# Placing the split activations of a down projection by a stepped offset, and reading part of its weights in interleaved chunks

## The chip, the cores and the metric

The kernel runs on one core of one Trainium2 chip. The metric is the device time of one execution in microseconds (us). Three executions of the kernel before took 2352.05, 2350.78 and 2352.41 us; their median is 2352.05 us.

## The reference

One layer of a diffusion backbone runs over 384 tokens (128 of a prompt and 256 latent ones) of 2048 channels: a mixer with three branches, then a gated feed-forward block whose hidden width is 5632. The change is in the last product of that block, the down projection, and in where the tiles behind it lie:

```python
h2 = rmsnorm(x, norm_ffn_pre) * (1 + sc2) + sh2
u, g = jnp.split(h2 @ w_ffn_up, 2, axis=-1)
g = along_cols(lambda t: dwconv(t, ffn_conv_w, ffn_conv_b), g, rows)
f = (jax.nn.gelu(g) * u) @ w_ffn_down
x = x + g2 * rmsnorm(f, norm_ffn_post)
```

All values are 32-bit floats. The kernel reaches the accuracy of a float32 product with three passes: an operand x is split into a rounded part hi and a rest lo, and a product is taken as hi·hi + lo·hi + hi·lo, each pass in the type fp32r.

## The kernel before

A long list of weight pieces is worked through in order (`run_stream`). Each piece of the down projection is one DMA of 128 rows by 1024 columns into a buffer `raw`. ScalarE (ACT) writes its rounded part `whi` and VectorE (DVE) its rest `wlo` (L164 and L165, in the helper `split`); three buffers of each take turns. Splits run two pieces ahead of the matmuls.

The down projection is the last stage. It has two halves of 1024 output columns (h = 0, 1), and in each half 44 steps (k = 0 to 43), one for each block of 128 hidden channels: 88 steps, numbered s = 44h + k. In a step the block `fx[k]` (128 channels by 384 tokens) is split into hi and lo as well (`down_split`, L1502 before), two steps ahead; here these are called the split activations. Then there are 18 matmuls: three groups of 128 tokens (t), two blocks of 512 columns (b), and three passes (L1512, L1513, L1514 before). In each the stationary operand, which a weight load (LDWEIGHTS, engine name PEld) brings into the array, is a 128x128 piece of the split activations, and the moving operand is 512 columns of `whi` or `wlo`. The sum stays in six PSUM banks over the 44 steps of a half. The last three steps of the second half (s = 85, 86, 87) are held back and run group by group in `down_last`, so that the work on a finished group (`down_out`, `down_finish`) runs beside the matmuls of the next one.

Where operands lie: the pool `hp` has 16 slots `hx0` to `hx15`, each a tile of 772 elements (3088 bytes) in every partition. In the built programs, before and after alike, neighbouring slots lie 3104 bytes apart, which is 32 bytes more than a multiple of 512. The buffers `whi` and `wlo` lie at multiples of 512 bytes from each other and from slot `hx0`. Before the change the split activations of step s are one tile in slot `hx{s % 3}`, with hi at its start and lo 1536 bytes (three times 512) behind it. So hi and lo of a step have the same place within 512 bytes, and against the weights that place is 0, 32 or 64 bytes on, by s % 3. "Offset" below means this: the address of the stationary operand less that of the moving one, within 512 bytes. It never changes within a step.

The stages before it run the other way round: in the input and up projections the stationary operand is a piece of `whi` or `wlo`, and the moving one is hi or lo of a normalised activation tile in slot `hx{k}`, k = 0 to 15 (L173, L174, L175). There the offset goes through 16 values that are 32 bytes apart, with the lo part 8 bytes further on. In the branch product that reads the tile `hc` all offsets are 0.

At the end of a half `down_out` squares each of the six PSUM banks into a scratch tile and multiplies it by a gain into a tile `fo` (128x512). Before, the twelve `fo` tiles of the two halves take slots `hx3` to `hx14`.

Of the kernel before, what the change touches and what calls it, by code (L numbers as in the profile page):

```python
# [12 lines left out]
F32 = mybir.dt.float32  # L13
F32R = mybir.dt.float32r
# [5 lines left out]
P = 128  # L20
# [4 lines left out]
NT = SEQ + LAT  # L25
HW = NT + 2
# [9 lines left out]
NF = DFF // P  # L36
# [10 lines left out]
NB = 512  # L47
# [45 lines left out]
def body(ctx: ExitStack, tc: tile.TileContext, i, o):  # L93
    nc = tc.nc
    ctx.enter_context(tc.manual_schedule())
    act, dve, pe, sync, gp = nc.scalar, nc.vector, nc.tensor, nc.sync, nc.gpsimd
# [10 lines left out]
    hp = ctx.enter_context(tc.tile_pool(name="hp", bufs=1, side="left"))  # L107
# [5 lines left out]
    def name(base):  # L113
        uid[0] += 1
        return f"{base}{uid[0]}"

    def bank(b, shape=(P, 512)):
        return psp.tile(list(shape), F32, name=name("ps"), tag=f"bank{b}")
# [44 lines left out]
    def split(hi, lo, src):  # L163
        act.activation(hi, src, AF.Copy)  # L164
        dve.tensor_sub(lo, src, hi.bitcast(F32))  # L165
# [126 lines left out]
    def sqrt_table():  # L292

        act.activation(tmp("dm", 1, bufs=1), eps, AF.Sqrt)
# [58 lines left out]
    hx = [None] * KD  # L353
# [4 lines left out]
    def h_pair(tag, n):  # L358

        t = hp.tile([P, 2, n], F32R, name=name("hx"), tag=tag)  # L360
        pr = Two()
        pr.hi, pr.lo = t[:, 0], t[:, 1]
        return pr
# [929 lines left out]
    F = {}  # L1293
# [167 lines left out]
    fo = {}  # L1461
# [30 lines left out]
    def g2_load(h):  # L1492
        t = F["p"].tile([P, 2, HALF_D], F32, name=name("gb"), tag="gb")
        for c in range(2):
            gp.dma_start(t[:, c], G2D[c : c + 1, HALF_D * h : HALF_D * (h + 1)].broadcast_to([P, HALF_D]))
        DN["g", h] = t

    def down_start():
        down_split(0)
        down_split(1)  # L1500

    def down_split(s):  # L1502
        if s >= 2 * NF:
            return
        pr = h_pair(f"hx{s % 3}", NT)
        split(pr.hi, pr.lo, fx[s % NF])
        DN["f", s] = pr

    def down_mm(ps, x, hi, lo, t, b, first, last):
        xh, xl = x.hi[:, t * P : (t + 1) * P], x.lo[:, t * P : (t + 1) * P]  # L1510
        w = slice(b * NB, (b + 1) * NB)
        pe.matmul(ps, xh, hi[:, w], start=first, stop=False, skip_group_check=True)  # L1512
        pe.matmul(ps, xl, hi[:, w], start=False, stop=False, skip_group_check=True)  # L1513
        pe.matmul(ps, xh, lo[:, w], start=False, stop=last, skip_group_check=True)  # L1514

    def down_use(h, k):
        def f(hi, lo):
            if k == 0:
                acc4 = [(rot["acc"] + c) % 4 for c in range(1, 5)]
                free = [4, 5, 6, 7] + acc4[:2] if h == 0 else acc4[2:] + [4, 5, 6, 7]  # L1520
                DN["ps", h] = [bank(b) for b in free]
            ps = DN["ps", h]
            x = DN.pop(("f", h * NF + k))
            down_split(h * NF + k + 2)
            if h == 1 and k >= NF - 3:
                DN["last"] = DN.get("last", []) + [(k, hi, lo, x)]
                if k == NF - 1:
                    down_last(ps)
                return
            for t in range(3):  # L1530
                for b in range(2):
                    down_mm(ps[2 * t + b], x, hi, lo, t, b, k == 0, k == NF - 1)
                if k == NF - 1:
                    for b in range(2):
                        down_out(h, t, b, ps[2 * t + b])
            if k == NF - 1:
                g2_load(1)
                sqrt_table()

        return f  # L1540

    def down_out(h, t, b, ps):

        n = 2 * h + b
        junk = hp.tile([P, NB], F32, name=name("junk"), tag="hx15")
        act.activation(junk, ps, AF.Square, accum_out=ss4[:, t, n : n + 1])
        g = hp.tile([P, NB], F32, name=name("fo"), tag=f"hx{3 + 4 * t + n}")
        dve.tensor_mul(g, ps, DN["g", h][:, min(t, 1), b * NB : (b + 1) * NB])
        fo[t, n] = g

    def down_last(ps):

        for t in range(3):
            for b in range(2):
                for k, hi, lo, x in DN["last"]:
                    down_mm(ps[2 * t + b], x, hi, lo, t, b, False, k == NF - 1)
                down_out(1, t, b, ps[2 * t + b])
                if b == 0:

                    sp = sp4[:, t : t + 1]  # L1560
                    dve.tensor_add(sp, ss4[:, t, 0:1], ss4[:, t, 1:2])
                    dve.tensor_add(sp, sp, ss4[:, t, 2:3])
                    dve.tensor_scalar(sp, sp, 1.0 / D, EPS, ALU.mult, ALU.add)
            if t:
                down_finish(t - 1)
        down_finish(2)
# [139 lines left out]
```

## Time and profile before

| | |
|---|---|
| median of three runs | 2352.05 us |
| the profiled execution's own time | 2352.14 us |
| its span, first to last instruction | 2350.4 us |
| mean granted TensorE clock | 0.995 |
| PE busy | 2312.1 us, 12597 matmuls |
| DVE busy, ACT busy | 1490.0 us, 933.8 us |
| down projection, matmuls L1512 to L1514 | 3 x 528, from 1970.4 to 2338.3 us |
| behind its last matmul | 12 us |

A timeline row has the start in us, the duration in us, the engine, the line, the operation and its tiles. Matmuls overlap in the records: one of 512 columns is recorded with 0.39 to 0.40 us, but the next begins about 0.23 us after it. So the time that a matmul costs is the distance between starts, called its **pitch** below, and not its recorded duration. Of a group, "x528 | 208.0, 394" means 528 instructions, 208.0 us in which at least one was busy, and 394 ns as the mean duration.

### The profile page before, as it was taken

How to read it: one execution, taken by the hardware profiler on the slowest of the kernel's cores; microseconds unless marked ns; L12 is line 12 of the kernel's file. 1: busy time of each engine (PE TensorE's matmuls, PEld its weight loads, DVE VectorE, ACT ScalarE, POOL GpSimd, SP SyncE). 2: the span in 40 equal slices, each digit the busy share in tenths (PEclk: the TensorE clock that was granted, in tenths of full speed). 3: DMA queues.
4: the chain of work that ended last, by engine and by line, in shares of the span. 5: the costliest groups of instructions: out<-in, count | busy, mean ns of one | idle time of the engine just before them, and what ended most of it. 6: DMA issues, size and time to landing. Idle time of an engine off the chain costs nothing.

```text
span 2350.4 us, 32026 instructions
## 1 busy us (share of the span) xinstructions
PE 2312.1 (98%) x12597; PEld 2189.8 (93%) x12597; DVE 1490.0 (63%) x2286; ACT 933.8 (40%) x1417; POOL 33.0 (1%) x72
## 2 busy tenths in 40 slices
PE   7999999999999999999999999999999999999997
PEld 3899999999999999999999999999999999888886
DVE  6876777646788777868556577776444445444444
ACT  6853333434322232324356533333333334334333
POOL 0000000000000000000000000000000000000000
PEclk9999999999999999999999999999999999999999
DMA  9954334234566666667533355554343333334332
GB/s 342 326 159 143 100 119 128 95 112 156 193 219 222 223 219 231 229 201 276 190 90 126 122 186 186 187 182 160 126 144 123 121 125 126 126 125 144 128 127 103
DMA packets 109335, 390.07 MB, mean 166 GB/s; under 512 B 12608, under 2 KB 12880, under 8 KB 109184
## 3 DMA queue, kind: packets, MB, share of 16 engines
q1 hardware_dynamic: 103968, 371.77, 47.6%
q0 software_dynamic: 4064, 14.36, 2.1%
q8 instruction: 98, 1.61, 0.3%
q10 hardware_dynamic: 1152, 1.90, 0.2%
q14 instruction: 53, 0.43, 0.1%
HBM read 382.71 MB, written 5.27 MB: 165 GB/s over the span
## 4 chain that ended last, share of the span: by engine, by line
PE 94%; DVE 2%; ACT 1%; DMA 1%; issue 1%; DVEq 0%; ACTq 0%; SPq 0%
PE ps L175 24%; PE ps L174 24%; PE ps L173 24%; PE ps L1513 5%; PE ps L1514 5%; PE ps L1512 5%; PE ps L897 1%; PE ps L899 1%; PE ps L898 1%; PE ps L400 1%; PE ps L994 1%; PE ps L989 1%; PE ps L401 1%; DMA eraw<-w_ada 0%; ACT ehi L164 0%
## 5 line engine op out<-in xcount | busy, mean ns | idle before, releaser
L165 DVE TENSOR_TENSOR wlo<-raw,whi 128x1024 fp32r<-128x1024 f32 (+2 forms) x520 | 622.5, 1199 | 755.0 <-ACT whi L164 754.8
L164 ACT ACTIVATE whi<-raw 128x1024 fp32r<-128x1024 f32 (+2 forms) x520 | 540.2, 1040 | 1272.3 <-PE ps L174 804.5
L173 PE MATMUL ps<-hx,whi 128*128 128x384 f32 (+1 forms) x3024 | 1026.7, 340 | 3.2 <-ACT hx L1316 3.2
L175 PE MATMUL ps<-hx,wlo 128*128 128x384 f32 (+1 forms) x3024 | 1026.6, 339 | 2.1 <-DVE wlo L165 2.1
L174 PE MATMUL ps<-hx,whi 128*128 128x384 f32 (+1 forms) x3024 | 1026.8, 340 | 0.1
L173 PEld LDWEIGHTS ps<-hx,whi 128*128 128x128 f32 x3024 | 571.5, 189 | 4.5 <-ACT hx L1316 3.4
L175 PEld LDWEIGHTS ps<-hx,wlo 128*128 128x128 f32 x3024 | 572.3, 189 | 3.5 <-DVE wlo L165 3.4
L174 PEld LDWEIGHTS ps<-hx,whi 128*128 128x128 f32 x3024 | 570.5, 189 | 1.8 <-DVE hx L165 0.4
L1177 DVE SCALAR_TENSOR_TENSOR cb<-raw,cb 128x1024 f32<-128x1024 f32 x256 | 313.1, 1223 | 9.2 <-DMA raw<-w_ada 3.3
L1513 PE MATMUL ps<-whi,hx 128*128 128x512 f32 x528 | 208.0, 394 | 0.8 <-DVE hx L165 0.8
L1514 PE MATMUL ps<-wlo,hx 128*128 128x512 f32 x528 | 208.2, 394 | 0.0
L1512 PE MATMUL ps<-whi,hx 128*128 128x512 f32 x528 | 207.8, 394 | 0.0
L1513 PEld LDWEIGHTS ps<-whi,hx 128*128 128x128 f32 x528 | 99.2, 188 | 24.4 <-DVE hx L165 1.1
L1512 PEld LDWEIGHTS ps<-whi,hx 128*128 128x128 f32 x528 | 99.2, 188 | 23.3 <-ACT hx L164 0.4
L1514 PEld LDWEIGHTS ps<-wlo,hx 128*128 128x128 f32 x528 | 99.2, 188 | 22.9
L165 DVE TENSOR_TENSOR elo<-eraw,ehi 128x1024 fp32r<-128x1024 f32 x56 | 66.9, 1221 | 22.8 <-ACT ehi L164 22.7
L712 DVE SCALAR_TENSOR_TENSOR cacc<-cbuf,vec,cacc 128x444 f32<-128x444 f32 x116 | 78.7, 679 | 2.8
L1404 DVE SCALAR_TENSOR_TENSOR t<-t,vec,t 128x192 f32<-128x192 f32 (+1 forms) x176 | 63.8, 383 | 16.1 <-ACT t L1395 12.9
L164 ACT ACTIVATE ehi<-eraw 128x1024 fp32r<-128x1024 f32 x56 | 56.3, 1047 | 18.8 <-DMA eraw<-w_ada 9.8
L897 PE MATMUL ps<-whi,hx 128*128 128x256 f32 x192 | 56.1, 292 | 0.0
L400 PE MATMUL ps<-ehi,cs 128*128 128x512 f32 x112 | 47.3, 422 | 6.9 <-ACT ehi L164 6.9
L898 PE MATMUL ps<-whi,hx 128*128 128x256 f32 x192 | 53.8, 280 | 0.0
(291 smaller groups left out, 1633.6 us busy)
## 6 DMA issues: line engine op xcount, KB each, us to landing
raw<-w_in SPq DMA_DIRECT2D x168, 512.0 KB, 3.9
raw<-w_up SPq DMA_DIRECT2D x164, 512.0 KB, 3.6
raw<-w_ada SPq DMA_DIRECT2D x128, 512.0 KB, 4.2
raw<-w_down SPq DMA_DIRECT2D x88, 512.0 KB, 3.2
eraw<-w_ada SPq DMA_DIRECT2D x64, 512.0 KB, 6.0
raw<-w_out SPq DMA_DIRECT2D x32, 512.0 KB, 4.6
raw<-w_v SPq DMA_DIRECT2D x16, 512.0 KB, 3.9
raw<-w_br SPq DMA_DIRECT2D x16, 512.0 KB, 4.9
```

Of the source, the lines that this page charges most:

```text
L164: act.activation(hi, src, AF.Copy)
L165: dve.tensor_sub(lo, src, hi.bitcast(F32))
L173: pe.matmul(out, wh, x, start=first, stop=False, skip_group_check=True)
L174: pe.matmul(out, wh, xl, start=False, stop=False, skip_group_check=True)
L175: pe.matmul(out, wl, x, start=False, stop=last, skip_group_check=True)
L712: dve.scalar_tensor_tensor(a, b[:, j : j + CPOS], w, a, ALU.mult, ALU.add)
L897: pe.matmul(outs[t], xh, hi[:, a], start=k == 0 and t != 1, stop=False, skip_group_check=True)
L898: pe.matmul(outs[t], xl, hi[:, a], start=False, stop=False, skip_group_check=True)
L1177: dve.scalar_tensor_tensor(MX["junk"], raw, 1.0, MX["cb"][c][half], ALU.mult, ALU.mult, accum_out=MODR[:, m, n, c, half : half + 1])
L1512: pe.matmul(ps, xh, hi[:, w], start=first, stop=False, skip_group_check=True)
L1513: pe.matmul(ps, xl, hi[:, w], start=False, stop=False, skip_group_check=True)
L1514: pe.matmul(ps, xh, lo[:, w], start=False, stop=last, skip_group_check=True)
```

## The change

It does three things.

The split activations of a step take two slots instead of one: hi lies in `hx{2r}` and lo in `hx{2r+1}`, with r = s % 3, so slots `hx0` to `hx5` are in use instead of `hx0` to `hx2`. Inside its slot a part starts `(32 * g - 16 * slot) % 512` bytes in, where g = 16s // 88 grows from 0 to 15 over the stage. If neighbouring slots lay 16 bytes off a multiple of 512, all parts of a step would have the one offset 32g. As they lie 32 bytes off it, hi is at the offset 32g + 32r and lo 16 bytes beyond it.

Of the steps s = 0 to 84, those with s % 5 = 2 read each block of 512 weight columns in another order: 16 columns of its first half, 16 of its second half, and so on in turn; those with s % 5 = 3 do so by 32 columns. The PSUM columns are written in the same order, so every sum is as before. That makes 17 steps of each kind and 54 steps as before, the last three among them.

The `fo` tiles of the first half go to slots `hx6` to `hx11`, and those of the second half to six of the tiles that held `fx`, which the stage has finished reading by then.

```diff
     def down_split(s):
         if s >= 2 * NF:
             return
-        pr = h_pair(f"hx{s % 3}", NT)
+        ring = s % 3
+        g = s * 16 // (2 * NF)
+        pr = Two()
+        for part in range(2):
+            slot = 2 * ring + part
+            off = (32 * g - 16 * slot) % 512 // 4
+            t = hp.tile([P, 2 * HW], F32R, name=name("hx"), tag=f"hx{slot}")[:, off : off + NT]
+            if part:
+                pr.lo = t
+            else:
+                pr.hi = t
         split(pr.hi, pr.lo, fx[s % NF])
         DN["f", s] = pr
 
-    def down_mm(ps, x, hi, lo, t, b, first, last):
+    def down_mm(ps, x, hi, lo, t, b, first, last, order=0):
         xh, xl = x.hi[:, t * P : (t + 1) * P], x.lo[:, t * P : (t + 1) * P]
         w = slice(b * NB, (b + 1) * NB)
-        pe.matmul(ps, xh, hi[:, w], start=first, stop=False, skip_group_check=True)
...
+        hi, lo = hi[:, w], lo[:, w]
+        if order:
+            ps, hi, lo = (z.rearrange("p (a b c) -> p b a c", c=order, a=2) for z in (ps, hi, lo))
+        pe.matmul(ps, xh, hi, start=first, stop=False, skip_group_check=True)
+        pe.matmul(ps, xl, hi, start=False, stop=False, skip_group_check=True)
+        pe.matmul(ps, xh, lo, start=False, stop=last, skip_group_check=True)
...
             x = DN.pop(("f", h * NF + k))
+            order = {2: 16, 3: 32}.get((h * NF + k) % 5, 0)
             down_split(h * NF + k + 2)
...
-                    down_mm(ps[2 * t + b], x, hi, lo, t, b, k == 0, k == NF - 1)
+                    down_mm(ps[2 * t + b], x, hi, lo, t, b, k == 0, k == NF - 1, order)
...
-        g = hp.tile([P, NB], F32, name=name("fo"), tag=f"hx{3 + 4 * t + n}")
+        if h == 0:
+            g = hp.tile([P, NB], F32, name=name("fo"), tag=f"hx{6 + 2 * t + n}")
+        else:
+            g = F["p"].tile([P, 3 * NT], F32, name=name("fo"), tag=f"f{2 * t + b}")[:, :NB]
```

On no engine does an instruction change its place; only line numbers, tiles and the shape of some matmuls differ. TensorE's rows at the end of step 1 and the start of step 2 were (output bank, weights, split activations, columns):

```order
L1514 MATMUL ps_17255<-wlo_17209,hx_17217 128x512
L1512 MATMUL ps_17250<-whi_17244,hx_17256 128x512
L1513 MATMUL ps_17250<-whi_17244,hx_17256 128x512
L1514 MATMUL ps_17250<-wlo_17245,hx_17256 128x512
L1512 MATMUL ps_17251<-whi_17244,hx_17256 128x512
L1513 MATMUL ps_17251<-whi_17244,hx_17256 128x512
L1514 MATMUL ps_17251<-wlo_17245,hx_17256 128x512
```

The same place of TensorE after the change; hi and lo are now two tiles, and the 512 columns are 16 times two chunks of 16:

```order
L1527 MATMUL ps_17257<-wlo_17209,hx_17218 128x512
L1525 MATMUL ps_17252<-whi_17246,hx_17258 128x16x2x16
L1526 MATMUL ps_17252<-whi_17246,hx_17259 128x16x2x16
L1527 MATMUL ps_17252<-wlo_17247,hx_17258 128x16x2x16
L1525 MATMUL ps_17253<-whi_17246,hx_17258 128x16x2x16
L1526 MATMUL ps_17253<-whi_17246,hx_17259 128x16x2x16
L1527 MATMUL ps_17253<-wlo_17247,hx_17258 128x16x2x16
```

What moved is the address of the stationary operand and the order of the columns within a matmul; the sequence of matmuls is the one before.

More of the change, by code (lines that the diff above doesn't have):

```diff
@@ L1504, in down_split @@
             return
-        pr = h_pair(f"hx{s % 3}", NT)
+        ring = s % 3
[9 more added lines that the diff above has]
+                pr.hi = t
         split(pr.hi, pr.lo, fx[s % NF])
         DN["f", s] = pr
-    def down_mm(ps, x, hi, lo, t, b, first, last):
+    def down_mm(ps, x, hi, lo, t, b, first, last, order=0):
         xh, xl = x.hi[:, t * P : (t + 1) * P], x.lo[:, t * P : (t + 1) * P]
         w = slice(b * NB, (b + 1) * NB)
-        pe.matmul(ps, xh, hi[:, w], start=first, stop=False, skip_group_check=True)
-        pe.matmul(ps, xl, hi[:, w], start=False, stop=False, skip_group_check=True)
-        pe.matmul(ps, xh, lo[:, w], start=False, stop=last, skip_group_check=True)
+        hi, lo = hi[:, w], lo[:, w]
[4 more added lines that the diff above has]
+        pe.matmul(ps, xh, lo, start=False, stop=last, skip_group_check=True)
     def down_use(h, k):
```

## The prediction

> **What bounds the kernel now.** I read the page's busy shares first, then the chain of work that ended last, then the timeline of the stage that the change touches. Busy times and chain of the kernel before:
>
> ```profile
> PE 2312.1 (98%) x12597; PEld 2189.8 (93%) x12597; DVE 1490.0 (63%) x2286; ACT 933.8 (40%) x1417; POOL 33.0 (1%) x72
> ...
> PE 94%; DVE 2%; ACT 1%; DMA 1%; issue 1%; DVEq 0%; ACTq 0%; SPq 0%
> PE ps L175 24%; PE ps L174 24%; PE ps L173 24%; PE ps L1513 5%; PE ps L1514 5%; PE ps L1512 5%; PE ps L897 1%; PE ps L899 1%; PE ps L898 1%; PE ps L400 1%; PE ps L994 1%; PE ps L989 1%; PE ps L401 1%; DMA eraw<-w_ada 0%; ACT ehi L164 0%
> ```
>
> TensorE is the bound: 94% of the chain is its matmuls, and the three lines of the down projection have about 5% each. What its matmuls wait for in that stage is in the groups by line:
>
> ```profile
> L1514 PE MATMUL ps<-wlo,hx 128*128 128x512 f32 x528 | 208.2, 394 | 0.0
> L1513 PE MATMUL ps<-whi,hx 128*128 128x512 f32 x528 | 208.0, 394 | 0.8 <-DVE hx L165 0.8
> L1512 PE MATMUL ps<-whi,hx 128*128 128x512 f32 x528 | 207.8, 394 | 0.0
> L1512 PEld LDWEIGHTS ps<-whi,hx 128*128 128x128 f32 x528 | 99.2, 188 | 23.3 <-ACT hx L164 0.4
> ```
>
> Within 1584 matmuls TensorE is idle 0.8 us. So the stage is worth its matmuls' count times their pitch, and the change can act on the pitch alone: it adds no matmul and takes none away. A weight load is recorded with 188 ns and lies beside the matmul before it.
>
> The pitch isn't constant. Below are the first matmuls of four steps that follow each other, s = 16, 17, 18 and 19, and from inside step 18 the ends of a run of 12 matmuls (timeline of TensorE):
>
> ```profile
> 2037.04 0.39 PE L1512 MATMUL ps<-whi,hx 128*128 128x512 f32 x1
> ...
> 2041.23 0.40 PE L1512 MATMUL ps<-whi,hx 128*128 128x512 f32 x1
> ...
> 2045.43 0.39 PE L1512 MATMUL ps<-whi,hx 128*128 128x512 f32 x1
> ...
> 2046.82 0.39 PE L1512 MATMUL ps<-whi,hx 128*128 128x512 f32 x1
> ...
> 2049.31 0.40 PE L1514 MATMUL ps<-wlo,hx 128*128 128x512 f32 x1
> 2049.55 0.39 PE L1512 MATMUL ps<-whi,hx 128*128 128x512 f32 x1
> ```
>
> Steps 16, 17 and 18 take 4.19, 4.20 and 4.12 us, or 232.8, 233.3 and 228.9 ns for each of 18 matmuls; the three together take 12.51 us, **231.7 ns** a matmul. They differ in one thing, the slot: offset 32, 64 and 0 bytes. In step 18 the run from 2046.82 to 2049.31 us has 11 pitches of **226.4 ns**, so its first matmuls still run at the pace of the step before and the rest are faster. Operations, shapes, clock and waits are alike; that leaves the offset as what sets these 5 to 7 ns.
>
> How much a matmul costs beyond its columns comes from a second size. In the branch product on `hc`, with 384 columns and offset 0 throughout, the first and the last of 24 matmuls are:
>
> ```profile
> 1064.14 0.33 PE L173 MATMUL ps<-hch,whi 128*128 128x384 f32 x1
> ...
> 1068.13 0.33 PE L175 MATMUL ps<-hch,wlo 128*128 128x384 f32 x1
> ```
>
> 3.99 us over 23 pitches is 173.5 ns. From 384 to 512 columns, at offset 0, the pitch grows by 226.4 - 173.5 = 52.9 ns, or 0.413 ns a column. So 512 columns are worth 211.5 ns, and 15 ns remain at offset 0 whatever the size. In steps 16 and 17 some 21 to 22 ns remain, and over the three slots 231.7 - 211.5 = 20.2 ns.
>
> **The change, part by part.** *Contiguous steps* (54 of 88, so 972 matmuls). Their offset now goes through all places, in steps of 16 and 32 bytes. The trace has one stage that does the same, the up projection: 16 slots, 32 bytes apart. One tile of it is 48 matmuls of 386 columns; here are two rows that lie 48 matmuls apart:
>
> ```profile
> 1939.69 0.34 PE L174 MATMUL ps<-hx,whi 128*128 128x386 f32 x1
> ...
> 1948.21 0.34 PE L174 MATMUL ps<-hx,whi 128*128 128x386 f32 x1
> ```
>
> 8.52 us over 48 is 177.5 ns; 386 columns are worth 159.5 ns, so 18.0 ns remain on average over all offsets. Put into the down projection this gives 211.5 + 18.0 = 229.5 ns in place of 231.7, a gain of 2.2 ns. The three slots in use before were a little worse than the average place. 972 x 2.2 ns is a gain of 2.1 us. The bounds: all at offset 0, 226.4 ns, is a gain of 5.2 us; all like step 17, 233.3 ns, is a loss of 1.6 us. That roles are exchanged there (weights stationary, activations moving) is why I keep both ends.
>
> *Interleaved steps* (34, so 612 matmuls). No matmul in the trace reads or writes in chunks. From below: the columns alone, 211.5 ns, a gain of 612 x 20.2 ns = 12.4 us. From above, by what a column costs: 32 or 16 chunks at up to two columns' time (0.83 ns) for each are 26 or 13 ns, on average 19.8 ns, a loss of 612 x 19.8 ns = 12.1 us. Farther up lies a load that no longer runs beside a matmul, 188 ns more each. I leave that out, as even the shortest products in three passes hide theirs:
>
> ```profile
> L898 PE MATMUL ps<-whi,hx 128*128 128x256 f32 x192 | 53.8, 280 | 0.0
> ```
>
> 280 ns is a recorded duration. In the down projection 394 ns go with a pitch of about 232, some 162 ns less, so these have about 118, under the 188 of a load. I take the value of the nearest row, the average over offsets: 229.5 ns again, a gain of 612 x 2.2 ns = 1.3 us.
>
> The Trainium skill speaks against this part: the page "PSUM — Partial Sum Buffer", section "Specifications (TRN2)", says of PSUM's 8-byte lines that "any non-contiguous AP slows matmuls significantly". No run here shows it; runs of 16 or 32 values fill whole such lines, but by the sentence as it stands this part is a loss.
>
> *Splits into two slots.* Each step still has one hi and one lo write, on engines that wait for TensorE and not the other way:
>
> ```profile
> L164 ACT ACTIVATE hx<-f 128x384 fp32r<-128x384 f32 x88 | 44.6, 508 | 0.0
> L165 DVE TENSOR_TENSOR hx<-f,hx 128x384 fp32r<-128x384 f32 x88 | 48.5, 552 | 0.0
> ...
> ACT whi L164 <- PE ps L1513: 221.5, 83, 2.7
> DVE wlo L165 <- ACT whi L164: 205.5, 85, 2.5
> ```
>
> ACT waits 221.5 us for TensorE in this stage, 2.7 us a step, and the split tiles still take turns three deep. Cost: nothing. If that cover were gone, what a step has there is 1.06 us, since ACT and DVE follow each other. At the stage's start four slots must be free instead of two. The up projection's last reads of `hx0` to `hx7` end before the splits begin:
>
> ```profile
> 1966.16 1.06 ACT L164 ACTIVATE whi<-raw 128x1024 fp32r<-128x1024 f32 x1 [2.79 <-PE ps L174]
> 1967.12 0.92 ACT L164 ACTIVATE hx<-f 128x384 fp32r<-128x384 f32 x2
> ```
>
> ACT begins that `whi` when TensorE is done with the piece that reads these slots, and the two splits stand behind it; the first down matmul starts 3.3 us later. No new wait.
>
> *Output tiles.* The same six writes a half, into places last read some 25 steps (about 100 us) earlier or in another stage. Nothing. The tail behind the last matmul keeps its 12 us, and the wait of 0.8 us at step 87 stays, since its slot and `whi` become free by the same matmuls as before.
>
> **Sum.** 2350.4 us of span, less 2.1 and 1.3, is 2347.0 us. The profiled execution took 1.7 us more than its span (2352.14), and the median of the runs is within 0.1 us of it. Forecast: **2348.7 us**, 0.14% below; a measurement of this kernel can tell about 0.2% (4.7 us) from no change.
>
> **Rivals.** *A, slower: chunks cost.* If each jump from one half of the block to the other holds the stream or the PSUM writes for about two columns' time, 612 matmuls lose 12.1 us; with the 2.1 us of the contiguous steps that is +10.0, **2362 us**. It decides from (4.7 + 2.1) / 612 = 11 ns a matmul on. For it: a pattern with three steps is new here, on both sides of the array. Against it: chunks of 64 and 128 bytes, and a column costs 0.41 ns throughout.
>
> *B, faster: chunks spare the meetings.* The 226.4 against 233.3 ns say that load and stream get in each other's way, by the place where they meet. The two halves of a block lie 1024 bytes apart, at the same place within 512, so an interleaved stream moves through places at half the pace and meets the load less often. If that halves the 15 ns that even offset 0 pays, the pitch is 219.0: 612 x 12.7 ns = 7.8 us, with 2.1 us **2342 us**. Against it: nothing shows that the 15 ns are meetings.
>
> *C: the offset is not what matters.* Then only the slot's absolute place made steps 16 to 18 differ, nothing is gained, **2352 us**. The Trainium skill stands here: "SBUF — State Buffer", section "SBUF: two separate sides", says that PE's port never waits on anyone, so offsets should be free. The trace disagrees, with 226.4 and 233.3 ns for the same instruction. A fact goes the same way: slots lie 3104 and not 3088 bytes apart, so the offsets are not the common one that the formula aims at. They still go through all places, and the average stands.
>
> **How the numbers follow.** Forecast 0.38, A 0.27, B 0.25, C 0.10. The forecast's own range, from its contiguous bounds and 3 ns either way on the interleaved ones, is 2344 to 2354, and 0.05 of its 0.38 lie beyond 0.2% faster. So faster 0.30, same 0.43 (0.33 and C's 0.10), slower 0.27. The range reaches past B and A, 2341 to 2363; about 0.1 lies above it, where chunks cost more than two columns' time, and 0.1 below, where B halves more than assumed.
>
> **What will show it.** The distances between the first matmuls of steps, by kind: 229.5 x 18 = 4.13 us for contiguous ones, with a spread from 4.08 to 4.20 over g, shows the offset at work; all alike shows C. Interleaved steps near 4.13 are the forecast; 4.37 and more lean to A (4.53 at its price), 3.95 and less to B. If 16-column steps lose twice what 32-column steps lose, the price is for the jump. A new wait of TensorE for ACT or DVE before s = 85 would show the split's cover wrong. The prediction falls if interleaved steps leave 3.95 to 4.37 us, or if contiguous ones average over 4.2.

## The result, and the profile after

| | before | after |
|---|---|---|
| median of 10 runs each | 2352.10 us | 2357.11 us |
| lowest to highest | 2350.78 to 2352.51 us | 2356.61 to 2357.38 us |
| span of the profiled execution | 2350.4 us | 2355.3 us |
| first to last down matmul, starts | 367.90 us | 372.47 us |
| behind the last down matmul's start | 12.1 us | 12.1 us |

The changed kernel takes 5.0 us more. The ratio after to before is 1.0022, with a 95% interval of 1.0012 to 1.0032. The forecast of 2348.7 us was on the wrong side. The time lies outside the forecast's own range (2344 to 2354 us) and inside the whole one (2341 to 2363 us), which reached past both rivals.

First the page of the kernel after: busy times, the chain by engine and, of the groups by line, the down projection's (L1525, L1526 and L1527 are what L1512, L1513 and L1514 were before).

```profile
PE 2316.7 (98%) x12597; PEld 2192.4 (93%) x12597; DVE 1490.6 (63%) x2286; ACT 933.8 (40%) x1417; POOL 33.0 (1%) x72
...
PE 94%; DVE 2%; ACT 1%; DMA 1%; issue 1%; DVEq 0%; ACTq 0%; SPq 0%
...
L1526 PE MATMUL ps<-whi,hx 128*128 128x512 f32 x528 | 209.3, 396 | 0.8 <-DVE hx L165 0.8
L1525 PE MATMUL ps<-whi,hx 128*128 128x512 f32 x528 | 209.8, 397 | 0.0
L1527 PE MATMUL ps<-wlo,hx 128*128 128x512 f32 x528 | 209.7, 397 | 0.0
```

The counts are the same, and TensorE is idle for the same 0.8 us. PE's busy time is 4.6 us more, and so is the time from the first to the last down matmul (372.47 - 367.90 = 4.57 us). So nothing waits for anything new: the stage's matmuls themselves come more slowly. Of the rest of the 4.9 us of span, 0.34 us had gone before the stage began, in stages that the change doesn't touch (first down matmul at 1970.73 us, before at 1970.40).

The timeline of TensorE shows which matmuls. These are the first ones of steps 0 to 5 after the change; step 2 reads by 16 columns, step 3 by 32.

```profile
1970.73 0.40 PE L1525 MATMUL ps<-whi,hx 128*128 128x512 f32 x1
...
1974.91 0.40 PE L1525 MATMUL ps<-whi,hx 128*128 128x512 f32 x1
...
1979.07 0.40 PE L1525 MATMUL ps<-whi,hx 128*128 128x512 f32 x1
...
1983.42 0.40 PE L1525 MATMUL ps<-whi,hx 128*128 128x512 f32 x1
...
1987.67 0.39 PE L1525 MATMUL ps<-whi,hx 128*128 128x512 f32 x1
...
1991.83 0.39 PE L1525 MATMUL ps<-whi,hx 128*128 128x512 f32 x1
```

The contiguous steps 0, 1 and 4 take 4.18, 4.16 and 4.16 us, step 2 takes 4.35 and step 3 takes 4.25 us. Over steps 0 to 84 the mean pitch (distance between starts, by the trace's records) is 232.2 ns in contiguous steps, 240.6 in 16-column steps and 235.8 in 32-column steps; before, it was 231.6 on average. With 306 matmuls of each interleaved kind that is 306 x 9.0 + 306 x 4.2 ns = 4.0 us, and some 0.5 us of the 4.57 are left for the contiguous steps.

### The profile page after: what moved, and what is told of

Read it like the earlier page. It is cut to its first block, busy times and chain, and to the rows that moved or that the text cites. A ratio compares the mean times of both kernels' runs of the same rounds, so it can differ in the third digit from the quotient of the medians.

```text
span 2355.3 us, 32026 instructions
## 1 busy us (share of the span) xinstructions
PE 2316.7 (98%) x12597; PEld 2192.4 (93%) x12597; DVE 1490.6 (63%) x2286; ACT 933.8 (40%) x1417; POOL 33.0 (1%) x72
## 3 DMA queue, kind: packets, MB, share of 16 engines
q10 hardware_dynamic: 1152, 1.90, 0.2%
## 4 chain that ended last, share of the span: by engine, by line
PE 94%; DVE 2%; ACT 1%; DMA 1%; issue 1%; DVEq 0%; ACTq 0%; SPq 0%
PE ps L175 24%; PE ps L174 24%; PE ps L173 24%; PE ps L1526 5%; PE ps L1527 5%; PE ps L1525 5%; PE ps L897 1%; PE ps L899 1%; PE ps L898 1%; PE ps L400 1%; PE ps L994 1%; PE ps L989 1%; PE ps L401 1%; DMA eraw<-w_ada 0%; ACT ehi L164 0%
## 5 line engine op out<-in xcount | busy, mean ns | idle before, releaser
L1526 PE MATMUL ps<-whi,hx 128*128 128x512 f32 x528 | 209.3, 396 | 0.8 <-DVE hx L165 0.8
L1525 PE MATMUL ps<-whi,hx 128*128 128x512 f32 x528 | 209.8, 397 | 0.0
L1527 PE MATMUL ps<-wlo,hx 128*128 128x512 f32 x528 | 209.7, 397 | 0.0
L1526 PEld LDWEIGHTS ps<-whi,hx 128*128 128x128 f32 x528 | 99.6, 189 | 25.4 <-DVE hx L165 1.1
L1527 PEld LDWEIGHTS ps<-wlo,hx 128*128 128x128 f32 x528 | 99.7, 189 | 24.3
L1525 PEld LDWEIGHTS ps<-whi,hx 128*128 128x128 f32 x528 | 99.6, 189 | 24.1 <-ACT hx L164 0.4
L897 PE MATMUL ps<-whi,hx 128*128 128x256 f32 x192 | 56.1, 292 | 0.0
```

Of the source, the lines that this page charges most:

```text
L897: pe.matmul(outs[t], xh, hi[:, a], start=k == 0 and t != 1, stop=False, skip_group_check=True)
L1525: pe.matmul(ps, xh, hi, start=first, stop=False, skip_group_check=True)
L1526: pe.matmul(ps, xl, hi, start=False, stop=False, skip_group_check=True)
L1527: pe.matmul(ps, xh, lo, start=False, stop=last, skip_group_check=True)
```

## The experiments

The question was twofold: what an offset costs, and what in an interleaved step costs 4 to 9 ns a matmul (the jumps in reading, the chunked PSUM writes, or something else). All edits are against the kernel after, unless a diff says otherwise. A pitch is a step's duration over 18, averaged over the steps of a kind. In the first matmuls of a step the pace of the step before goes on; where that matters, the pitch at the step's end is given as "steady". Except for `zero`, these kernels have one timed execution each, and the readings rest on the trace, where, within a run, steps of the same kind, offset and slot that follow on the same kind of step agree within some 15 ns of about 4200.

### Each part of the change alone: ilv_only and off_only

`off_only` drops the interleaving:

```diff
-            order = {2: 16, 3: 32}.get((h * NF + k) % 5, 0)
+            order = 0
```

> The changed kernel without interleaving: the offsets as its formula gives them, hi and lo 16 bytes apart. Theory I: all steps average the 232.2 ns that the contiguous steps of the changed kernel have; 1584 x 0.5 ns is 0.8 us, a span near 2351.2 us. Rival: an average of 234 ns or more and a span of 2354 us or more. By the prediction's own step it would have been 229.5 ns and 2347 us.

`ilv_only` keeps the interleaving and puts the split activations back into their three slots:

```diff
-        ring = s % 3
-        g = s * 16 // (2 * NF)
...
+        pr = h_pair(f"hx{s % 3}", NT)
         split(pr.hi, pr.lo, fx[s % NF])
```

> The kernel before, with the interleaved reading alone added (the split activations in their old places). Theory I (the interleaved steps carry the loss, wherever the activations lie): 16-column steps 240 to 242 ns a matmul, 32-column steps 235 to 237, and the others as before, 228.9 to 233.3 by slot; 306 x 9 + 306 x 4 ns = 4.0 us, so a span near 2354.5 us. Rival (the offsets carry it, or both only together): a span within 1.5 us of 2350.4.

| first to last down matmul | us | against before |
|---|---|---|
| before | 367.90 | |
| off_only | 368.77 | +0.87 |
| ilv_only | 371.56 | +3.66 |
| after | 372.47 | +4.57 |

0.87 + 3.66 = 4.53 us: the two parts add up to the whole, and interleaving is four fifths of it. In `ilv_only` the pitch is 231.4 ns in contiguous steps, 240.0 in 16-column steps and 235.7 in 32-column steps, so interleaving costs about as much in the old slots as in the new ones. Step against step (`ilv_only` against before, the kernel after against `off_only`), every one of the 34 interleaved steps takes longer than the same step read in order, by 1.4 to 12.9 ns a matmul.

### No offset at all: zero

All split activations at offset 0, nothing interleaved. Since slots lie 32 bytes off a multiple of 512, the formula with 32 in place of 16 takes that out:

```diff
-            off = (32 * g - 16 * slot) % 512 // 4
+            off = (-32 * slot) % 512 // 4
...
-            order = {2: 16, 3: 32}.get((h * NF + k) % 5, 0)
+            order = 0
```

> The changed kernel without interleaving, and with all split activations, hi and lo of every step, at offset 0 to the weights. Theory O (the offset sets the pitch): all 88 steps run like the fast part of step 18 before, 226.4 to 226.7 ns a matmul, 4.08 us a step; against 231.7 that is 1584 x 5 ns = 8 us less, a span near 2342.5 us and a time near 2344 us. Rival P (the absolute place of a slot, not its offset to the weights, made step 18 fast): slots hx2 to hx5 are slow whatever their offset, two steps in three stay at 4.19 to 4.20 us, and the time stays within 2 us of 2352.

Six runs have a median of 2344.21 us (2343.64 to 2344.97), beside 2351.96 us for ten runs of the kernel before: the ratio is 0.9967, interval 0.9955 to 0.9979. The page of `zero` has for the engines' busy times:

```profile
PE 2303.8 (98%) x12597; PEld 2189.5 (93%) x12597; DVE 1490.2 (64%) x2286; ACT 933.8 (40%) x1417; POOL 33.0 (1%) x72
```

PE is busy 8.3 us less than before, with the same 12597 matmuls. In the timeline of TensorE its steps 1, 2 and 3 start here:

```profile
1973.84 0.39 PE L1525 MATMUL ps<-whi,hx 128*128 128x512 f32 x1
...
1977.92 0.39 PE L1525 MATMUL ps<-whi,hx 128*128 128x512 f32 x1
...
1982.00 0.39 PE L1525 MATMUL ps<-whi,hx 128*128 128x512 f32 x1
```

Every step behind the first takes 4.08 us, 226.7 ns a matmul, whichever of the six slots it uses. So which slot it is doesn't matter; where the operand begins does. This kernel beats the one before by 7.8 us and, by the medians, the one after by 12.9.

`whi` and `wlo` always lie at multiples of 512 bytes, so this run can't tell the offset between the operands from the stationary operand's own place. The up projection of the trace before speaks for more than the latter: there the weights are stationary and keep their place, the activations move through the slots, and the pitch follows the slot. Over 60 tiles its median is 174.7 ns at k = 3 and k = 11, and 180.0 ns at k = 5 and k = 13; slots eight apart, whose places lie 256 bytes apart, agree to 0.1 ns in all eight pairs. So the place of either operand counts. That their difference alone does isn't shown, as no run moves both.

### A true common offset: scan_common

```diff
-            off = (32 * g - 16 * slot) % 512 // 4
+            off = (32 * g - 32 * slot) % 512 // 4
...
-            order = {2: 16, 3: 32}.get((h * NF + k) % 5, 0)
+            order = 0
```

> The changed kernel without interleaving, with its formula mended: hi and lo of a step at one common offset 32g, g from 0 to 15 over the stage, 5 to 6 steps at each. Theory O: steps at one g agree and the g differ; 4.08 us at g = 0, near 4.20 us at g = 1 and 2, and an average of all g near 229.5 ns a matmul (4.13 us a step), as the prediction took from the up projection. Rival (the up projection's average does not hold for exchanged roles): an average of 231 to 233 ns, as in the contiguous steps of the changed kernel (232.2). Rival P: steps go by slot in threes and not by g.

It took 2352.19 us. The table has the mean pitch at each common offset (without the first step of a half, which carries the pace of what came before):

| offset 32g, bytes | 0 | 32 | 64 | 96 | 128 | 160 | 192 | 224 |
|---|---|---|---|---|---|---|---|---|
| pitch, ns | 226.7 | 233.2 | 233.3 | 234.2 | 232.4 | 233.3 | 229.0 | 233.4 |
| 256 bytes further | 226.7 | 233.2 | 233.3 | 234.2 | 232.4 | 233.3 | 229.0 | 233.4 |

The starts of steps 34 and 35 (offset 192) and 50 and 51 (offset 288) of `scan_common`:

```profile
2112.06 0.39 PE L1525 MATMUL ps<-whi,hx 128*128 128x512 f32 x1
...
2116.18 0.39 PE L1525 MATMUL ps<-whi,hx 128*128 128x512 f32 x1
...
2178.18 0.39 PE L1525 MATMUL ps<-whi,hx 128*128 128x512 f32 x1
...
2182.38 0.40 PE L1525 MATMUL ps<-whi,hx 128*128 128x512 f32 x1
```

They take 4.12 and 4.20 us. The pattern repeats every 256 bytes, not 512, and offset 0 is one of the two best places of sixteen. The mean is 231.9 ns: going through all places gains nothing over the three slots of before (231.6). The prediction had 229.5 for this mean.

### Finer offsets: fine

```diff
-        g = s * 16 // (2 * NF)
+        g = s * 32 // (2 * NF)
...
-            off = (32 * g - 16 * slot) % 512 // 4
+            off = (8 * g - 32 * slot) % 512 // 4
...
-            order = {2: 16, 3: 32}.get((h * NF + k) % 5, 0)
+            order = 0
```

> As the scan of common offsets, but in steps of 8 bytes from 0 to 248, 2 or 3 steps at each, contiguous. Theory O with places that are wide (a neighbouring 8 or 16 bytes act as one): values near 0 (8, 248) stay at 226.7 to 228 ns and the change to 233 lies somewhere below 32; the average stays near 231.8. If each 8 bytes count by themselves: 8 and 248 are already near 233, and a few places may lie below 226.7.

It took 2353.55 us. Steps of 8 bytes matter by themselves: 0 gives 226.7 ns, 8 gives 230.8, 16 gives 233.3, 24 gives 230.0, and from 32 to 72 all lie between 233.2 and 233.4. The lowest between are 226.9 at 120 (two steps), 230.0 at 24 and 228.3 at 240; the highest is 234.4 at 96. The mean is 232.2 ns. No place read is better than 0 (248 falls into the last steps, which run group by group). So neither expectation came quite: 8 isn't near 0, and not near 233 either.

The offset alone doesn't fix the pace. At 192 `scan_common` has 229.0 ns, in both halves of the 512 bytes, and `fine`, which ran on another chip, has 233.4 with the same matmuls at the same offset. `off_only` shows the like within one run. These are the starts of steps 67 and 68 (offset 192) of `fine`, and then those of steps 3, 4, 80 and 81 of `off_only`; its steps 3 and 80 both have hi at offset 0 and lo at 16:

```profile
2251.00 0.40 PE L1525 MATMUL ps<-whi,hx 128*128 128x512 f32 x1
...
2255.20 0.40 PE L1525 MATMUL ps<-whi,hx 128*128 128x512 f32 x1
```

```profile
1983.40 0.39 PE L1525 MATMUL ps<-whi,hx 128*128 128x512 f32 x1
...
1987.49 0.39 PE L1525 MATMUL ps<-whi,hx 128*128 128x512 f32 x1
...
2305.27 0.39 PE L1525 MATMUL ps<-whi,hx 128*128 128x512 f32 x1
...
2309.44 0.40 PE L1525 MATMUL ps<-whi,hx 128*128 128x512 f32 x1
```

They take 4.20, 4.09 and 4.17 us. Steps 3 and 80 follow on other offsets (64 and 224 bytes) and use other slots; whether the pace before or the slot decides between two paces isn't shown. Contiguous steps with both parts at offset 0 came to 226.7 ns in every run, behind whatever step.

### Why the up projection's average didn't carry over: scan384

`scan_common` with 384 of the 512 weight columns in every matmul but those of a half's first step:

```diff
         hi, lo = hi[:, w], lo[:, w]
+        if not first:
+            hi, lo, ps = hi[:, :NT], lo[:, :NT], ps[:, :NT]
```

> The scan of common offsets with 384 of each 512 columns (the last quarter of each block's columns is left out, save in the first step of a half). It asks why the up projection's remainder of 18 ns did not carry over to the down projection, whose average over offsets left 20.3 ns. If the number of columns makes it: on average near 159 + 18 = 177 ns here too, as with 386 columns there. If it is the roles (weights moving, activations loaded) or that an offset stays the same from matmul to matmul: 173.5 at offset 0 and near 180 elsewhere, 179 on average.

It took 2264.91 us. The pitch by offset, again the same in both halves of the 512 bytes and without the first step of a half:

| offset, bytes | 0 | 32 | 64 | 96 | 128 | 160 | 192 | 224 | mean |
|---|---|---|---|---|---|---|---|---|---|
| 384 columns, ns | 173.6 | 173.4 | 174.7 | 176.6 | 176.0 | 176.6 | 173.4 | 176.7 | 175.0 |
| 512 columns, ns | 226.7 | 233.2 | 233.3 | 234.2 | 232.4 | 233.3 | 229.0 | 233.4 | 231.9 |

With the same operands in the same roles, the average over offsets lies 1.6 ns above the best place at 384 columns (175.0 against 173.4) and 5.2 ns at 512. So the remainder isn't one number that a size only adds columns to: at offset 32 it is nothing over the best place at 384 columns, and 6.5 ns at 512. Neither expected average came (177 if the columns make it, 179 if the roles do); 175.0 is lower than both, and why the up projection has 177.5 at 386 columns stays open.

The trace before had a third size in these very roles: the product of 256 columns (L897 to L899) has activations from all 16 slots as stationary operands. Its starts lie 117.7 ns apart on average. So the average pitch over places is 117.7, 175.0 and 231.9 ns at 256, 384 and 512 columns, and at 0.413 ns a column 12, 16 and 20 ns remain. The remainder grows with the columns, where the prediction held it fixed.

### Which chunks cost: chunks

At offset 0 throughout (as in `zero`), with five sizes of chunks beside contiguous steps:

```diff
-            off = (32 * g - 16 * slot) % 512 // 4
+            off = (-32 * slot) % 512 // 4
...
-            order = {2: 16, 3: 32}.get((h * NF + k) % 5, 0)
+            order = (0, 8, 16, 32, 64, 128)[(h * NF + k) % 6]
```

> All split activations at offset 0, and by s % 6 the weights are read contiguously, or in chunks of 8, 16, 32, 64 and 128 columns. In the changed kernel 16-column steps took 240.6 and 32-column steps 235.8 ns a matmul, where 231.7 was the pitch before: 9 and 4 ns, or 0.28 and 0.26 ns for each of 32 or 16 chunks. Theory J (a price for each chunk): on top of 226.5 ns, 64 chunks of 8 give 243 to 244 ns, then 235, 231, 229 and 227.5 ns. Rival M (interleaving changes where load and stream meet): no line through the number of chunks; a chunk size that stays within one place costs nothing and another one more, and at offset 0 the 16-column steps need not lie above contiguous ones at all.

It took 2354.82 us. The starts of steps 6 to 12, whose kinds are contiguous, 8, 16, 32, 64, 128, contiguous:

```profile
1995.52 0.39 PE L1525 MATMUL ps<-whi,hx 128*128 128x512 f32 x1
...
1999.60 0.40 PE L1525 MATMUL ps<-whi,hx 128*128 128x512 f32 x1
...
2003.98 0.41 PE L1525 MATMUL ps<-whi,hx 128*128 128x512 f32 x1
...
2008.30 0.40 PE L1525 MATMUL ps<-whi,hx 128*128 128x512 f32 x1
...
2012.56 0.40 PE L1525 MATMUL ps<-whi,hx 128*128 128x512 f32 x1
...
2016.66 0.39 PE L1525 MATMUL ps<-whi,hx 128*128 128x512 f32 x1
...
2020.74 0.39 PE L1525 MATMUL ps<-whi,hx 128*128 128x512 f32 x1
```

| columns in a chunk | whole | 128 | 64 | 32 | 16 | 8 |
|---|---|---|---|---|---|---|
| chunks in a matmul | 1 | 4 | 8 | 16 | 32 | 64 |
| mean pitch, ns | 226.7 | 226.6 | 227.8 | 236.6 | 240.2 | 243.2 |
| over contiguous | | 0 | 1.1 | 9.9 | 13.5 | 16.5 |

A price per chunk would double from column to column. Twice the chunks (16 to 32 to 64) bring only 3.6 and 3.0 ns more, and 8 chunks are free: the 1.1 ns are carried over from the 32-column step before, in the first three pitches (237, 233 and 230 ns in step 10), and from the fourth on the pitch is 226.7. So chunks of 64 columns cost nothing and chunks of 32 do. 64 columns are 256 bytes, the length after which the offsets repeat.

### Reading or writing: read_write

At offset 0, chunks on one side alone: the weights are read interleaved and the PSUM is written straight, or the other way round (so columns of the result change places).

```diff
...
+            f = lambda z: z.rearrange("p (a b c) -> p b a c", c=abs(order), a=2)
+            if order > 0:
+                hi, lo = f(hi), f(lo)
+            else:
+                ps = f(ps)
...
+            order = (0, 16, -16, 32, -32)[(h * NF + k) % 5]
```

> All split activations at offset 0. By s % 5: contiguous; only the weights are read in chunks of 16; only PSUM is written in chunks of 16; only read in 32; only written in 32. So output columns are permuted in these steps and the output is not the reference's. Theory W (the price is on PSUM's side, chunks written apart): write-only steps cost 8 to 9 ns (16) and 4 ns (32) a matmul over 226.5, read-only ones nothing. Theory R (the price is on the read side, a jump or a meeting with the load): read-only steps cost that much, write-only ones nothing. If both add up, each takes a part.

It took 2353.05 us. Timeline of `read_write`: the starts of steps 5 (contiguous), 6 (read by 16), 7 (written by 16), a matmul inside step 7, and the starts of steps 8 (read by 32) and 9 (written by 32):

```profile
1991.28 0.39 PE L1529 MATMUL ps<-whi,hx 128*128 128x512 f32 x1
...
1995.36 0.40 PE L1529 MATMUL ps<-whi,hx 128*128 128x512 f32 x1
...
1999.68 0.39 PE L1529 MATMUL ps<-whi,hx 128*128 128x512 f32 x1
...
2002.45 0.39 PE L1529 MATMUL ps<-whi,hx 128*128 128x512 f32 x1
...
2003.81 0.40 PE L1529 MATMUL ps<-whi,hx 128*128 128x512 f32 x1
...
2008.07 0.40 PE L1529 MATMUL ps<-whi,hx 128*128 128x512 f32 x1
```

Step 6 takes 4.32 us and step 8 takes 4.26: 240.0 and 236.5 ns on average over their kinds, the whole price of the chunks. Step 7 takes 4.13 us, and its last six pitches (2002.45 to 2003.81) are 1.36 us, 226.7 ns each: only its first matmuls still carry the pace of step 6. Writing PSUM in chunks of 16 or 32 costs nothing; the cost is in the reading.

### Is it the jumps: places

At offset 0, PSUM contiguous, 16 columns at a time, in three orders: the two halves in turn; 32 chunks in fours, each 320 bytes behind the one before, and every four begin 256 bytes behind the last four's start, so that the stream jumps but goes on through the places within 256 bytes in sequence; eight eighths in turn.

```diff
...
+        if order == 4:
+            hi, lo = (dataclasses.replace(z, ap=[list(z.ap[0]), [64, 8], [80, 4], [1, 16]], offset=z.offset + 256 * b) for z in (hi0, lo0))
+            ps = ps.rearrange("p (a b c) -> p a b c", a=8, c=16)
+        elif order:
+            hi, lo = (z.rearrange("p (a b c) -> p b a c", c=16, a=order) for z in (hi, lo))
...
+            order = (0, 2, 4, 8)[(h * NF + k) % 4]
```

> All split activations at offset 0, PSUM written contiguously; by s % 4 the weights are read contiguously; 16 columns from each half in turn; in 32 chunks of 16 columns that lie 320 bytes apart, so that the stream jumps at every chunk and still goes on through the places within 256 bytes as a contiguous one does (other columns of the block are read, some twice); and 16 columns from each of eight eighths in turn, so that it stays at one place within 256 bytes for eight chunks. Outputs aren't the reference's. Theory M (the pace through the places within 256 bytes, against that of the load, sets the cost): 226.7, 240, 226.7 to 228 ns, and for the eighths another number, above 240 if it grows as the pace falls. Theory J (a jump of the read costs): all three chunked kinds near 240 ns, as each has 32 chunks.

It took 2355.42 us. Timeline of `places`: the starts of steps 4 to 7 in that order (contiguous, halves, jumps in sequence, eighths), one matmul late in step 6 and the start of step 8:

```profile
1986.62 0.40 PE L1530 MATMUL ps<-whi,hx 128*128 128x512 f32 x1
...
1990.73 0.40 PE L1530 MATMUL ps<-whi,hx 128*128 128x512 f32 x1
...
1995.05 0.40 PE L1530 MATMUL ps<-whi,hx 128*128 128x512 f32 x1
...
1997.81 0.39 PE L1530 MATMUL ps<-whi,hx 128*128 128x512 f32 x1
...
1999.17 0.40 PE L1530 MATMUL ps<-whi,hx 128*128 128x512 f32 x1
...
2003.48 0.40 PE L1530 MATMUL ps<-whi,hx 128*128 128x512 f32 x1
```

Halves in turn: 4.32 us, 240.0 ns on average over the kind. Eighths in turn: 4.31 us, 239.4. The jumps that keep the sequence end at 1.36 us for six, 226.7 ns, after a run-in. So 32 jumps in a matmul cost nothing by themselves. What costs is a reading order that leaves the sequence of places within 256 bytes. This fits `chunks`: halves in turn by 64 or 128 columns keep that sequence. Eight chunks at one place are no dearer than two.

### Is it the return to the same place: returns

16 columns from each of two parts in turn, the second part 1024, 1088, 1152 or 1216 bytes behind the first. Only at 1024 does the second chunk lie at the first one's place within 256 bytes.

```diff
...
+            hi, lo = (dataclasses.replace(z, ap=[list(z.ap[0]), [16, 16], [256 + order - 1, 2], [1, 16]], offset=z.offset + 256 * b) for z in (hi0, lo0))
+            ps = ps.rearrange("p (a b c) -> p a b c", b=2, c=16)
...
+            order = (0, 1, 17, 33, 49)[(h * NF + k) % 5]
```

> All split activations at offset 0, PSUM written contiguously; by s % 5 the weights are read contiguously, or 16 columns in turn from two halves whose distance is 1024, 1088, 1152 or 1216 bytes (the last three read other columns, so outputs aren't the reference's). Within 256 bytes the second chunk of a pair then lies 0, 64, 128 or 192 bytes on. Theory Q (the stream pays when a chunk starts at the place where the chunk before it was): 226.7, then 240 at 1024 and at 1088 (there the next pair begins where this one ended), and below 230 at 1152 and 1216, where no chunk follows one at its own place. Rival H (the halved pace through the places is what costs): all four near 240.

It took 2362.14 us. The starts of steps 6 to 10 of `returns` (the four distances in that order, then contiguous):

```profile
1996.49 0.40 PE L1528 MATMUL ps<-whi,hx 128*128 128x512 f32 x1
...
2000.81 0.40 PE L1528 MATMUL ps<-whi,hx 128*128 128x512 f32 x1
...
2005.13 0.41 PE L1528 MATMUL ps<-whi,hx 128*128 128x512 f32 x1
...
2009.45 0.40 PE L1528 MATMUL ps<-whi,hx 128*128 128x512 f32 x1
...
2013.78 0.40 PE L1528 MATMUL ps<-whi,hx 128*128 128x512 f32 x1
```

All four take 4.32 to 4.33 us; the means are 240.1, 240.0, 240.2 and 240.4 ns. So a chunk at the place of the one just before isn't what costs. Every order tried that doesn't walk steadily through the places gave about 240 ns at 16 columns, and the one that does gave 227.

### Is it the meeting with the weight load: half_load

Offset 32; contiguous and by 16 columns, each with a stationary operand of 128 and of 64 columns (so half of every token group is left out in the latter).

```diff
...
+        m = P // 2 if order % 2 else P
+        xh, xl, ps = x.hi[:, t * P : t * P + m], x.lo[:, t * P : t * P + m], ps[0:m]
+        order -= order % 2
...
-            off = (32 * g - 16 * slot) % 512 // 4
+            off = (32 - 32 * slot) % 512 // 4
...
-            order = {2: 16, 3: 32}.get((h * NF + k) % 5, 0)
+            order = (0, 1, 16, 17)[(h * NF + k) % 4]
```

> All split activations at offset 32, where a contiguous matmul takes 233.3 ns and a 16-column one about 241. By s % 4: contiguous; contiguous with a stationary operand of 64 columns instead of 128 (so half the output rows are left out); 16-column chunks; 16-column chunks with 64 columns. Theory L (what is paid over the columns is the stream meeting the weight load): half the load lets a contiguous matmul fall from 233.3 to 225 or less and a 16-column one from 241 to 230 or less. Rival S (the moving stream pays by itself, for instance by coming back to a place too soon): 64 columns change nothing, within 2 ns.

It took 2358.22 us. The weight loads of one line, in the groups by line and form of `half_load` over the stage:

```profile
L1527 PEld LDWEIGHTS ps<-whi,hx 128*128 128x128 f32 x269 | 51.0, 189 | 15.1 <-ACT hx L164 0.4
L1527 PEld LDWEIGHTS ps<-whi,hx 128*64 128x64 f32 x252 | 34.5, 137 | 23.2
```

The load is 52 ns shorter with 64 columns. From the timeline of `half_load`, the starts of steps 4 (contiguous, 128), 5 (contiguous, 64), 6 (by 16, 128), 7 (by 16, 64) and 8:

```profile
1986.53 0.40 PE L1527 MATMUL ps<-whi,hx 128*128 128x512 f32 x1
...
1990.72 0.39 PE L1527 MATMUL ps<-whi,hx 128*64 128x512 f32 x1
...
1994.89 0.40 PE L1527 MATMUL ps<-whi,hx 128*128 128x512 f32 x1
...
1999.21 0.40 PE L1527 MATMUL ps<-whi,hx 128*64 128x512 f32 x1
...
2003.53 0.40 PE L1527 MATMUL ps<-whi,hx 128*128 128x512 f32 x1
```

Contiguous steps gain 2 ns (233.2 to 231.3 on average), interleaved ones nothing (240.0 and 240.0). The theory that the stream meets the load had asked for 225 and 230 or less, so in that form it falls. 52 of 189 ns is 28%, and 1.9 ns is 29% of the 6.5 ns that offset 32 costs: for contiguous steps a price that grows with the load's length would fit, on this one pair of numbers. For interleaved steps it doesn't: 28% of their 13.3 ns over offset 0 would be 3.7 ns, and none of it went. That doesn't rule out a meeting whose price hangs on something other than the load's length. At 16 columns the interleaved pitch at offset 32 is 240.0 as it is at offset 0, and in `ilv_only` it lies between 239.8 and 240.1 in all three slots. By 32 columns the offset still counts: there `ilv_only` has 234.2 ns at offset 32 and 236.3 to 236.4 at offsets 0 and 64.

## Why the prediction failed, point by point

**TensorE is the bound, and only the pitch can move: right.** Idle time, counts, load times and the 12.1 us of tail are as before.

**The offset sets the pitch: right in the main.** The prediction read 226.4 ns from 11 pitches inside one step; `zero` has 226.7 in every step behind the first, and moving the same instructions 32 bytes costs 6.5 ns. The rival that the offset doesn't matter falls. So, for this case, does what the prediction drew under it from the Trainium skill ("SBUF — State Buffer", section "SBUF: two separate sides"), that offsets should be free. But one offset can have two paces (`fine`), which no part of the prediction allowed for.

**Contiguous steps, -2.1 us: failed, +0.5 us.** By `off_only` the new offsets cost 0.87 us over all 1584 matmuls; the share of these 972 is 0.53. The step that failed: "so 18.0 ns remain on average over all offsets", taken at 386 columns and added to the 211.5 ns of 512. `scan384` shows that what an offset costs changes with the columns: on average 16 ns remain at 384 and 20 at 512. A row that the prediction shows itself, the 256 columns with about 118 ns, leaves 12 and spoke against a fixed remainder. The bounds (-5.2 to +1.6 us) held, and they used rows of 512 columns only.

**Interleaved steps, -1.3 us: failed, +4.0 us.** 3.7 us are for the chunks and 0.3 for the new offsets. The step that failed: "I take the value of the nearest row, the average over offsets". That row is a contiguous read, and the thing to be priced was a read that isn't. The bounds (-12.4 to +12.1 us) held, with a middle that no row supported.

**Rival A had the sign, not the mechanism.** It asked for 19.8 ns a matmul, from jumps or PSUM writes. Measured are 9.0 and 4.2 ns over before. Jumps that keep the sequence are free (`places`), and so are chunked PSUM writes (`read_write`). The sentence of the Trainium skill that was cited against the change ("PSUM — Partial Sum Buffer", section "Specifications (TRN2)") forecast the sign rightly, but these runs don't show its effect: for chunks of 16 and 32 values PSUM writes keep 226.7 ns.

**Rival B, interleaving spares meetings, falls:** step against step every interleaved one was slower, at the old offsets as at the new ones.

**Two tests of the prediction were too weak.** Contiguous steps average 4.18 us (it wanted over 4.2 to fall) and interleaved ones 4.25 and 4.33 (it wanted 4.37), so by its own marks it would have stood, though 612 matmuls at 6.6 ns more (the mean of 9.0 and 4.2) turn the sign. And "if 16-column steps lose twice what 32-column steps lose, the price is for the jump": they do (9.0 against 4.2 ns), and it isn't. The ratio only looks like two because the base, 231.6 ns, already holds 5 ns of offset; from the base at offset 0 it is 13.5 against 9.9 (`chunks`).

**No new wait, splits and output tiles free: right.** TensorE's one wait in the stage is the same 0.8 us.

**Sum.** The forecast's span was 2347.0 us, and 2355.3 was measured, 8.3 us more: 2.6 from the contiguous steps (2.1 + 0.5), 5.3 from the interleaved ones (1.3 + 4.0), and 0.3 from a later start of the stage; the rest is rounding.

What stays open is why an order that leaves the sequence costs what it does: whether the stream pays by itself or where it meets the load, and why the pitch is about 240 ns for all such orders at 16 columns. No run separates the two. Open as well is what picks the pace where one offset has two.

## What to carry to other kernels

When a stage is bound by matmuls, look at the distance between their starts step by step. If it changes with nothing but a tile's place, try to bring both operands to the same address within 256 bytes; here that is worth 5 ns of 232 on each matmul of 512 columns, and 7.8 us in all. Check where tiles really lie: the formula of this change assumed slots 16 bytes apart where they lie 32, but even its true form gained nothing, since of the eight places 32 bytes apart one is best and an average over all isn't. Keep the moving operand contiguous, or in chunks of 64 or 128 columns (256 or 512 bytes), the two sizes that cost nothing here, and don't price an operation that the trace lacks by the nearest row that isn't that operation.

## What the runs showed that was not expected

The effect of the offset repeats every 256 bytes and shows in steps of 8. Many offsets and orders settle at one of three values, 226.7, 233.3 and 240.0 ns, which lie 6.7 ns apart. At 384 columns the best is 173.4 ns, 53.3 under 226.7, which is eight times as much. One offset can hold two paces (229.0 and 233.4 ns at 192). An interleaved step at 16 columns is at 240.0 ns at offset 0 and 32 alike, with a short load as with a long one. And the pace of a step goes on into the next: behind a 240 ns step, a 226.7 ns step comes to its own pace late (in step 6 of `places` the first 12 pitches, from 1995.05 to 1997.81 us, average 230.0 ns).
